# Gate and up products of two feed-forward stages by Strassen's scheme, down products in blocks of two pairs

## The chip, the cores and the metric

The kernel runs on one core of a Trainium2 chip. The metric is the device time of one execution in microseconds; the median of several runs is compared. The engines of the core are PE (TensorE: matmuls, with PEld for its weight loads), DVE (VectorE), ACT (ScalarE), POOL (GpSimd) and SP (SyncE, which issues most DMAs). Each engine executes its own instructions in a fixed order and waits on semaphores for the others.

## The reference, cut to what matters

The reference runs a two-layer block (convolutions, attentions, a mixture of 16 experts) and then a second block on 512 tokens of width 1024. The second block begins and ends with a feed-forward stage, and these two stages are what the change touches:

```python
D_MODEL = 1024; SEQ = 512; D_FF = 2816

def swiglu(x, w_gate, w_up, w_down):
    return (jax.nn.silu(x @ w_gate) * (x @ w_up)) @ w_down

def hybrid_layer(x, positions, layer_idx, ...):
    x = x + 0.5 * swiglu(rms_norm_2(x, ffn1_norm), ffn1_w_gate, ffn1_w_up, ffn1_w_down)
    ...                      # mixers
    x = x + 0.5 * swiglu(rms_norm_2(x, ffn2_norm), ffn2_w_gate, ffn2_w_up, ffn2_w_down)
    return x
```

All data are fp32. `x @ w_gate` and `x @ w_up` are each 512 x 1024 times 1024 x 2816; the product with `w_down` is 512 x 2816 times 2816 x 1024.

## The kernel before

**Precision.** A product of two fp32 matrices is made of three matmuls of a shorter type, fp32r. An operand is split into a part `hi`, which ACT makes by a copy that rounds to fp32r, and a rest `lo = x - hi`, by a subtraction on DVE or POOL (`split`, L307 to L311; `take_hl`, L253 to L265, for weights that come by DMA). `mm3` (L321 to L325) then issues hi times hi, hi times lo and lo times hi into one PSUM accumulator; its three matmuls are lines L323, L324 and L325.

**A stage** (`ffn`, L1610). The activations lie transposed in `hT`: eight blocks k of 128 channels by 512 tokens, hi and lo. `D_FF` = 2816 is 11 "pairs" p of two blocks q of 128 columns. Per pair the gate weights and the up weights come as one DMA each, 128 x 8 x 256 fp32, 1 MB. `take_hl` splits each into hi and lo, in two halves of 128 x 1024. Per block q, PE makes the gate product in a PSUM tile of pool `pd` and the up product in one of pool `pa`, each by 8 x 3 matmuls with the weights stationary (128 x 128) and 512 tokens moving. DVE scales the gate product by the row `rb` (1 / rms of each token), ACT takes the silu, DVE scales the up product and multiplies the two, and `split` leaves hi and lo in `fh` and `fl`. After 6 pairs, and again after the other 5, the down product follows: per half h of the output columns, 12 (then 10) blocks f of 128 rows of `w_down` arrive in three DMAs, and for each of 4 token tiles t, PE accumulates over all f in a PSUM tile of pool `pb`; DVE adds half of the sum to x (L1652). `along` makes `rb` on the way, in the first pair; `first_scale` also rescales x in the first stage. `rope_angles`, which the mixers need later, is issued beside the first down product of the first stage. `after(0)` and `after(1)` begin the next step (squares, transposes) when a half of x is ready.

**Which engine subtracts.** In the first stage `self.dve` is False, and the second half of each weight's `lo` is subtracted on POOL; before the second stage it is set True (`FDVE`), and DVE subtracts both halves.

**Buffers.** Weights and their hi and lo parts share the pool `wp` of 6 buffers of 8 KB per partition. `pump` (L235) lets at most `cap` = 2 weights be issued that are not yet released; `rel` releases.

**Order.** Instructions are written in program order, and a planner of the framework lays down a fixed order for each engine: it plays the program through with its own costs, and an engine that is free takes the ready instruction that stands first in the program. On the chip that order is kept, whatever the real durations.

The functions of the diff and what calls them, with the lines of the profile:

Of the kernel before, what the change touches and what calls it, by code (L numbers as in the profile page):

```python
# [6 lines left out]
F32 = mybir.dt.float32  # L7
# [62 lines left out]
YHB = 2  # L70
NEG = -1.0e30
# [46 lines left out]
class Kern:  # L118
# [327 lines left out]
    def block2_entries(self):  # L446
        def ffn(i):
            for f0, nf in ((0, 6), (6, 5)):
# [3 lines left out]
                for h in range(2):  # L452
                    r = 2 * f0 * 128
                    for n in (2 * nf - 8, 4, 4):
                        self.entries.append(([n, 512], self.a[f"f{i}d"][r:r + n * 128, h * 512:(h + 1) * 512]
                                             .rearrange("(k p) f -> p k f", p=128), "d"))
                        r += n * 128
# [1151 lines left out]

    def ffn(self, N, scale, after, beside=None):  # L1610
# [3 lines left out]
        es = self.phase(t2p=8)  # L1614
        hT = N["hT"]
        ef = self.phase(hf=1)
        fh = self.one(self.hf, (12, 512), F32R, "fh")
        fl = self.one(self.hf, (12, 512), F32R, "fl")
        rb = None
        for nf in (12, 10):  # L1620
            for p in range(nf // 2):
                Wg = self.take_hl()
                Wu = self.take_hl()
                for q in range(2):
# [4 lines left out]
                    if rb is None:  # L1629
                        rb = self.along(self.hf, scale())  # L1630
# [5 lines left out]
                    self.split(s, fh[:, 2 * p + q], fl[:, 2 * p + q], nc.vector)  # L1636
            for h in range(2):
                acc = [self.pb((2, 512)) for _ in range(2)]
                f0 = 0
                for q, n in enumerate((nf - 8, 4, 4)):  # L1640
                    W = self.take_hl()
                    if beside and (q, h) == (0, 1):
                        beside()
                        beside = None
                    for t in range(NX):
                        for f in range(n):
                            ff = f0 + f
                            self.mm3(acc[t // 2][:, t % 2], [z[:, ff, t * 128:(t + 1) * 128] for z in (fh, fl)],
                                     [w[:, f] for w in W], ff == 0, ff == nf - 1)
                        if q == 2:  # L1650
                            xs = self.xt(t)[:, h * 512:(h + 1) * 512]
                            nc.vector.scalar_tensor_tensor(xs, acc[t // 2][:, t % 2], 0.5, xs, op0=ALU.mult, op1=ALU.add)  # L1652
                    f0 += n
                    if nf == 10 and h == 1 and q == 0:
                        after(0)
# [443 lines left out]
```

## Time and profile before

| | before |
|---|---|
| median of 3 runs | 3044.39 us (3040.3, 3044.39, 3051.68) |
| profiled execution, its own time | 3035.68 us |
| its span | 3033.9 us |
| PE busy | 2839.7 us (94%) |
| DVE busy | 1276.4 us (42%) |
| ACT busy | 825.6 us (27%) |
| POOL busy | 467.5 us (15%) |
| mean granted TensorE clock | 0.97 of 2.4 GHz |

The span runs from the first to the last instruction. Busy is the time in which an engine has an instruction in work; the matmuls of PE overlap, so the distance from one matmul's start to the next, not its own duration, says how fast PE goes. The first feed-forward stage lies at about 1876 to 2220 us of the span, the second at about 2649 to 3024 us.

### The profile page before, as it was taken

How to read it: one execution, taken by the hardware profiler on the slowest of the kernel's cores; microseconds unless marked ns; L12 is line 12 of the kernel's file. 1: busy time of each engine (PE TensorE's matmuls, PEld its weight loads, DVE VectorE, ACT ScalarE, POOL GpSimd, SP SyncE). 2: the span in 40 equal slices, each digit the busy share in tenths (PEclk: the TensorE clock that was granted, in tenths of full speed). 3: DMA queues.
4: the chain of work that ended last, by engine and by line, in shares of the span. 5: the costliest groups of instructions: out<-in, count | busy, mean ns of one | idle time of the engine just before them, and what ended most of it. 6: DMA issues, size and time to landing. Idle time of an engine off the chain costs nothing.

```text
span 3033.9 us, 38589 instructions
## 1 busy us (share of the span) xinstructions
PE 2839.7 (94%) x15736; PEld 1800.9 (59%) x15736; DVE 1276.4 (42%) x2623; ACT 825.6 (27%) x1531; POOL 467.5 (15%) x380
## 2 busy tenths in 40 slices
PE   6989899999999898997999888999999999999998
PEld 3666675444444365574433224787886777788786
DVE  4387744111111157743222225532447483444344
ACT  4266432000000135631000003322236442322222
POOL 2233332111110132331000000221210001100000
PEclk9999899999999899898999999999999999999999
DMA  7710137999999842057999996222231122222222
GB/s 269 271 69 15 42 111 277 405 403 404 400 403 388 315 152 98 29 194 289 419 420 419 420 420 281 83 101 94 88 105 56 65 85 87 93 95 98 84 90 77
DMA packets 103842, 623.13 MB, mean 205 GB/s; under 512 B 11056, under 2 KB 13232, under 8 KB 36592
## 3 DMA queue, kind: packets, MB, share of 16 engines
q1 hardware_dynamic: 89120, 580.82, 48.6%
q0 software_dynamic: 8352, 18.10, 2.3%
q10 hardware_dynamic: 6192, 21.75, 1.9%
q8 instruction: 124, 2.03, 0.3%
q14 instruction: 54, 0.44, 0.0%
HBM read 601.74 MB, written 18.87 MB: 205 GB/s over the span
## 4 chain that ended last, share of the span: by engine, by line
PE 40%; DMA 11%; DVE 2%; ACT 1%; issue 0%; SPq 0%; DVEq 0%; ACTq 0%; POOLq 0%
PE pd L323 6%; PE pd L324 5%; PE pd L325 5%; DMA w<-w_up 4%; DMA w<-w_down 3%; DMA w<-w_gate 3%; PE pb L323 3%; PE pb L325 3%; PE pb L324 3%; PE pa L323 3%; PE pa L324 3%; PE pa L325 3%; PE pb L1223 2%; PE pd L1260 1%; PE pb L1791 1%; DVE wl L263 1%
## 5 line engine op out<-in xcount | busy, mean ns | idle before, releaser
L1223 PE MATMUL pb<-w,X 128*64 128x512 f32 x2048 | 463.2, 597 | 19.8 <-DMA w<-w_up 10.5
L1223 PEld LDWEIGHTS pb<-w,X 128*64 128x64 f32 x2048 | 149.5, 137 | 316.0 <-issue 265.5
L262 ACT CAST wh<-w 128x1024 fp32r<-128x1024 f32 (+3 forms) x239 | 235.8, 1028 | 367.9 <-issue 126.7
L1260 PE MATMUL pd<-w,hT 128*64 128x512 f32 (+1 forms) x2048 | 301.1, 490 | 5.2 <-DVE hT L319 2.6
L323 PE MATMUL pd<-hh,wh 128*128 128x512 f32 (+1 forms) x720 | 285.7, 397 | 10.6 <-ACT wh L262 6.4
L263 DVE TENSOR_TENSOR wl<-w,wh 128x1024 fp32r<-128x1024 f32 (+2 forms) x187 | 229.9, 1248 | 147.5 <-ACT wh L262 142.9
L324 PE MATMUL pd<-hl,wh 128*128 128x512 f32 (+1 forms) x720 | 285.1, 396 | 0.0
L325 PE MATMUL pd<-hh,wl 128*128 128x512 f32 (+1 forms) x720 | 284.2, 395 | 0.3 <-DVE wl L263 0.3
L1233 ACT ACTIVATE s<-pb 128x512 f32<-128x512 f32 x32 | 19.1, 597 | 695.8 <-PE pb L1223 695.8
L263 POOL TENSOR_TENSOR wl<-w,wh 128x1024 fp32r<-128x1024 f32 (+1 forms) x52 | 137.4, 2642 | 423.8 <-ACT wh L262 418.4
L1260 PEld LDWEIGHTS pd<-w,hT 128*64 128x64 f32 (+1 forms) x2048 | 101.9, 123 | 163.8 <-issue 129.7
L1234 DVE TENSOR_TENSOR s<-s,pb 128x512 f32<-128x512 f32 x32 | 22.0, 686 | 390.6 <-ACT s L1233 390.6
L323 PEld LDWEIGHTS pd<-hh,wh 128*128 128x128 f32 x720 | 138.7, 193 | 40.7 <-ACT wh L262 9.8
L325 PEld LDWEIGHTS pd<-hh,wl 128*128 128x128 f32 x720 | 138.9, 193 | 29.3 <-DVE wl L263 1.0
L324 PEld LDWEIGHTS pd<-hl,wh 128*128 128x128 f32 x720 | 139.3, 193 | 28.2 <-issue 1.4
L323 PE MATMUL pb<-wh,fh 128*128 128x512 f32 x352 | 139.2, 400 | 0.8 <-DVE x L1652 0.8
L323 PE MATMUL pa<-hh,wh 128*128 128x512 f32 x352 | 139.5, 396 | 0.0
L324 PE MATMUL pa<-hl,wh 128*128 128x512 f32 x352 | 139.5, 396 | 0.0
L325 PE MATMUL pa<-hh,wl 128*128 128x512 f32 x352 | 139.5, 396 | 0.0
L325 PE MATMUL pb<-wh,fl 128*128 128x512 f32 x352 | 139.2, 396 | 0.0
L324 PE MATMUL pb<-wl,fh 128*128 128x512 f32 x352 | 138.9, 395 | 0.0
L1191 POOL DMA_INDIRECT gat<-xd,gi x48 | 46.8, 974 | 575.5 <-PE pa L1205 326.5
(459 smaller groups left out, 4713.0 us busy)
## 6 DMA issues: line engine op xcount, KB each, us to landing
w<-w_up SPq DMA_DIRECT2D x128, 1024.0 KB, 17.2
w<-w_gate SPq DMA_DIRECT2D x128, 1024.0 KB, 16.8
w<-w_down SPq DMA_DIRECT2D x128, 1024.0 KB, 19.2
w<-ada_w SPq DMA_DIRECT2D x48, 1024.0 KB, 5.3
w<-w_in SPq DMA_DIRECT2D x18, 1024.0 KB, 7.0
w<-f1g SPq DMA_DIRECT2D x11, 1024.0 KB, 5.0
w<-f1u SPq DMA_DIRECT2D x11, 1024.0 KB, 4.9
w<-f2g SPq DMA_DIRECT2D x11, 1024.0 KB, 4.9
```

The source lines that it names most:

```text
L262: nc.scalar.copy(hi[:, s], w[:, s])
L263: (nc.gpsimd if i and not (dve or self.dve) else nc.vector).tensor_tensor(lo[:, s], w[:, s], hi[:, s].bitcast(F32), op=ALU.subtract)
L323: nc.tensor.matmul(ps, lhsT=l[0], rhs=r[0], start=first, stop=False)
L324: nc.tensor.matmul(ps, lhsT=l[0], rhs=r[1], start=False, stop=False)
L325: nc.tensor.matmul(ps, lhsT=l[1], rhs=r[0], start=False, stop=last)
L1191: self.nc.gpsimd.indirect_dma_start(out=g, out_offset=None, in_=R["xd"].rearrange("t (h w) -> (t h) w", h=dup), in_offset=bass.IndirectOff ...
L1223: nc.tensor.matmul(pp[h * cap:(h + 1) * cap, 0:w], lhsT=X[:, k], rhs=Wk[:, h * w:(h + 1) * w], start=(k == 0), stop=(k == 7))
L1233: nc.scalar.activation(out=s, in_=pp[:, 0, 0:w], func=AF.Silu)
L1234: nc.vector.tensor_tensor(s, s, pp[:, 1, 0:w], op=ALU.mult)
L1260: nc.tensor.matmul(py[h * cap:(h + 1) * cap, 0:w], lhsT=hT[:, k % nj, k // nj], rhs=Wd[k // 2][:, k % 2, h * w:(h + 1) * w], start=(k == 0 ...
L1791: nc.tensor.matmul(s_[:, g, :nk], lhsT=qT[0:96, h, n * 128:nk], rhs=kT[0:96, h, 0:nk], start=True, stop=False)
```

## The change

Both operands of the gate and up products are cut into quarters: the weights of a pair by k (blocks 0 to 3 and 4 to 7) and by q, the activations by k and by tokens (0 to 255 and 256 to 511). Strassen's scheme (in Winograd's form) makes the four quarters of the result of 7 products of quarters, where the direct way takes 8. Every product is 4 blocks k times 3 matmuls, 256 tokens wide.

- Pair 0 of each stage stays as it was. Beside it, `crossed` adds hi and lo of the activations to fp32 again and forms three combined quarters on POOL, which are split into hi and lo; `cross` then replaces one quarter of `hT` in place, on DVE and ACT.
- Pairs 1 to 10 go through `ffn_pair`. `seven` makes the 7 weight quarters of a matrix one after the other: four sums on POOL (128 x 512 each), and a split of each quarter, hi on ACT and lo on DVE, into a pool `pr` of 5 buffers; `sq` has 4 buffers for the sums. Gate and up products alternate. Each product goes to one half (256 columns) of a PSUM bank: four halves in two tiles per matrix, used in turn. The results are added up by ACT (the first) and DVE into four SBUF tiles of the pool `t2p`, which shrinks from 8 to 6 buffers. The two scalings by `rb` are both on the gate side, one on DVE and one, after the silu, on POOL.
- The down product follows after every second pair (and after the last alone), over 4 (the last: 2) blocks f, with one DMA of weights per half h. Its result is added to x six times in a stage instead of twice.
- `rope_angles` is issued after pair 0, `after(0)` after the first half of the last down product.

```diff
@@ -68,6 +68,9 @@
 ORATE = 1
 OCAP = 1
 YHB = 2
+SQ = 4
+PR = 5
+FT2 = 6
 NEG = -1.0e30
 TWO_PI = 6.283185307179586
 LAM_INIT = 0.8 - 0.6
@@ -445,16 +448,14 @@
 
     def block2_entries(self):
         def ffn(i):
-            for f0, nf in ((0, 6), (6, 5)):
+            for f0 in range(0, 11, 2):
+                nf = min(2, 11 - f0)
                 for p in range(f0, f0 + nf):
                     self.dense_entries(f"f{i}g", None, p, p + 1, (8, 256))
                     self.dense_entries(f"f{i}u", None, p, p + 1, (8, 256))
                 for h in range(2):
-                    r = 2 * f0 * 128
-                    for n in (2 * nf - 8, 4, 4):
-                        self.entries.append(([n, 512], self.a[f"f{i}d"][r:r + n * 128, h * 512:(h + 1) * 512]
-                                             .rearrange("(k p) f -> p k f", p=128), "d"))
-                        r += n * 128
+                    self.entries.append(([2 * nf, 512], self.a[f"f{i}d"][2 * f0 * 128:2 * (f0 + nf) * 128, h * 512:(h + 1) * 512]
+                                         .rearrange("(k p) f -> p k f", p=128), "d"))
         ffn(1)
         self.dense_entries("z0", None, 0, 2, (4, 416))
         self.dense_entries("wuq", None, 0, 1, (2, 768))
@@ -1607,18 +1608,123 @@
             nc.vector.scalar_tensor_tensor(self.xt(t), self.xt(t), r[:, t:t + 1], self.row, op0=ALU.mult, op1=ALU.mult)
         return r2
 
+    def crossed(self, N):
+        nc = self.nc
+        hi, lo = N["hi"], N["lo"]
+        T4 = self.xy.tile([128, 2, 4, 256], F32R, name=self.nm("T4"), tag="xyc", bufs=1)
+        T23 = [self.one(self.hf, (2, 4, 256), F32R, f"T{i}") for i in (2, 3)]
+        a, b = slice(0, 256), slice(256, 512)
+        for k in range(4):
+            f1, f2, c, d = (self.t2() for _ in range(4))
+            for f, kk in ((f1, k), (f2, k + 4)):
+                nc.gpsimd.tensor_tensor(f, hi[:, kk].bitcast(F32), lo[:, kk].bitcast(F32), op=ALU.add)
+            nc.gpsimd.tensor_tensor(c[:, a], f2[:, b], f1[:, b], op=ALU.subtract)
+            nc.gpsimd.tensor_tensor(f1[:, b], f1[:, b], f1[:, a], op=ALU.subtract)
+            nc.gpsimd.tensor_tensor(c[:, b], f2[:, b], f1[:, b], op=ALU.subtract)
+            nc.gpsimd.tensor_tensor(d[:, a], f2[:, a], c[:, b], op=ALU.subtract)
+            for T, z in ((T23[0], c[:, b]), (T23[1], c[:, a]), (T4, d[:, a])):
+                self.split(z, T[:, 0, k], T[:, 1, k], nc.vector)
+        return T23[0], T23[1], T4
+    def cross(self, N):
+        nc = self.nc
+        hi, lo = N["hi"], N["lo"]
+        for k in range(4):
+            f = self.t2()
+            nc.vector.tensor_tensor(f, hi[:, k].bitcast(F32), lo[:, k].bitcast(F32), op=ALU.add)
+            nc.vector.tensor_tensor(f[:, 0:256], f[:, 256:512], f[:, 0:256], op=ALU.subtract)
+            self.split(f[:, 0:256], hi[:, k, 256:512], lo[:, k, 256:512], nc.vector)
+    def seven(self, w):
+        nc = self.nc
+        A = lambda f, K: w[:, 4 * K:4 * K + 4, 128 * f:128 * f + 128]
+        s = self.one(self.sq, (4, 128), s="sq")
+        def pair(z):
+            t = self.one(self.pr, (2, 4, 128), F32R, "pr")
+            self.split(z, t[:, 0], t[:, 1], nc.vector)
+            return t
+        yield pair(A(0, 0))
+        nc.gpsimd.tensor_tensor(s, A(1, 0), A(1, 1), op=ALU.add)
+        s2 = self.one(self.sq, (4, 128), s="sq")
+        nc.gpsimd.tensor_tensor(s2, s, A(0, 0), op=ALU.subtract)
+        yield pair(s2)
+        yield pair(s)
+        yield pair(A(0, 1))
+        nc.gpsimd.tensor_tensor(A(1, 0), A(0, 0), A(1, 0), op=ALU.subtract)
+        yield pair(A(1, 0))
+        nc.gpsimd.tensor_tensor(s2, A(0, 1), s2, op=ALU.subtract)
+        yield pair(s2)
+        yield pair(A(1, 1))
+    def ffn_pair(self, N, T, rb, out):
+        nc = self.nc
+        hi, lo = N["hi"], N["lo"]
+        q = lambda K, t: [z[:, 4 * K:4 * K + 4, 256 * t:256 * t + 256] for z in (hi, lo)]
+        c = lambda z: [z[:, i] for i in range(2)]
+        rhs = [q(0, 0), c(T[0]), q(0, 1), q(1, 0), c(T[1]), q(1, 1), c(T[2])]
+        M = []
+        for pool in (self.pd, self.pa):
+            w = self.take()
+            M.append(dict(F=self.seven(w), ps=[z[:, h * 256:h * 256 + 256] for z in (pool(), pool()) for h in range(2)],
+                          r=[self.t2() for _ in range(2)]))
+        a, b = slice(0, 256), slice(256, 512)
+        add = lambda o, x, y: nc.vector.tensor_tensor(o, x, y, op=ALU.add)
+        mul = lambda o, x, y, e=nc.vector: e.tensor_tensor(o, x, y, op=ALU.mult)
+        for i in range(7):
+            for up, m in enumerate(M):
+                l = next(m["F"])
+                ps = m["ps"][i % 4]
+                for k in range(4):
+                    self.mm3(ps, [l[:, j, k] for j in range(2)], [r[:, k] for r in rhs[i]], k == 0, k == 3)
+                r0, r1 = m["r"]
+                if i == 0:
+                    nc.scalar.copy(r0[:, a], ps)
+                elif i == 1:
+                    add(r1[:, b], ps, r0[:, a])
+                elif i == 2:
+                    add(r0[:, b], ps, r1[:, b])
+                elif i == 3:
+                    add(r0[:, a], ps, r0[:, a])
+                elif i == 4:
+                    add(r1[:, a], ps, r1[:, b])
+                    add(r1[:, b], ps, r0[:, b])
+                else:
+                    h = i - 5
+                    r, c = (r0, b) if h == 0 else (r1, a)
+                    add(r[:, c], ps, r[:, c])
+                    if not up:
+                        mul(r, r, rb)
+                        nc.scalar.activation(out=r, in_=r, func=AF.Silu)
+                        mul(r, r, rb, nc.gpsimd)
+                    else:
+                        mul(r, r, M[0]["r"][h])
+                        out(h, r)
+        for m in M:
+            next(m["F"], None)
+        self.rel(2)
     def ffn(self, N, scale, after, beside=None):
 
         MARK("ffn")
         nc = self.nc
-        es = self.phase(t2p=8)
+        es = self.phase(t2p=FT2)
         hT = N["hT"]
         ef = self.phase(hf=1)
-        fh = self.one(self.hf, (12, 512), F32R, "fh")
-        fl = self.one(self.hf, (12, 512), F32R, "fl")
-        rb = None
-        for nf in (12, 10):
-            for p in range(nf // 2):
+        eo = None
+        for p in range(11):
+            if p % 2 == 0:
+                F = []
+            z = self.one(self.hf, (2, 2, 512), F32R, "fh", bufs=3)
+            F.append(z)
+            out = lambda q, s, z=z: self.split(s, z[:, 0, q], z[:, 1, q], nc.vector)
+            if p == 0:
                 Wg = self.take_hl()
                 Wu = self.take_hl()
                 for q in range(2):
@@ -1626,33 +1732,37 @@
                     for W, pp in ((Wg, pg), (Wu, pu)):
                         for k in range(8):
                             self.mm3(pp, [w[:, k, q * 128:(q + 1) * 128] for w in W], [h[:, k] for h in hT], k == 0, k == 7)
-                    if rb is None:
+                    if q == 0:
                         rb = self.along(self.hf, scale())
                     g, s = self.t2(), self.t2()
                     nc.vector.tensor_tensor(g, pg, rb, op=ALU.mult)
                     nc.scalar.activation(out=g, in_=g, func=AF.Silu)
                     nc.vector.tensor_tensor(s, pu, rb, op=ALU.mult)
                     nc.vector.tensor_tensor(s, s, g, op=ALU.mult)
-                    self.split(s, fh[:, 2 * p + q], fl[:, 2 * p + q], nc.vector)
+                    out(q, s)
+                if beside:
+                    beside()
+                T = self.crossed(N)
+                self.cross(N)
+                eo = self.phase(sq=SQ, pr=PR)
+            else:
+                self.ffn_pair(N, T, rb, out)
+            if p % 2 == 0 and p < 10:
+                continue
+            nf = 2 * len(F)
+            if p == 10:
+                eo.close()
             for h in range(2):
                 acc = [self.pb((2, 512)) for _ in range(2)]
-                f0 = 0
-                for q, n in enumerate((nf - 8, 4, 4)):
-                    W = self.take_hl()
-                    if beside and (q, h) == (0, 1):
-                        beside()
-                        beside = None
-                    for t in range(NX):
-                        for f in range(n):
-                            ff = f0 + f
-                            self.mm3(acc[t // 2][:, t % 2], [z[:, ff, t * 128:(t + 1) * 128] for z in (fh, fl)],
-                                     [w[:, f] for w in W], ff == 0, ff == nf - 1)
-                        if q == 2:
-                            xs = self.xt(t)[:, h * 512:(h + 1) * 512]
-                            nc.vector.scalar_tensor_tensor(xs, acc[t // 2][:, t % 2], 0.5, xs, op0=ALU.mult, op1=ALU.add)
-                    f0 += n
-                    if nf == 10 and h == 1 and q == 0:
-                        after(0)
+                W = self.take_hl()
+                for t in range(NX):
+                    for f in range(nf):
+                        self.mm3(acc[t // 2][:, t % 2], [F[f // 2][:, i, f % 2, t * 128:(t + 1) * 128] for i in range(2)],
+                                 [w[:, f] for w in W], f == 0, f == nf - 1)
+                    xs = self.xt(t)[:, h * 512:(h + 1) * 512]
+                    nc.vector.scalar_tensor_tensor(xs, acc[t // 2][:, t % 2], 0.5, xs, op0=ALU.mult, op1=ALU.add)
+                if p == 10 and h == 0:
+                    after(0)
         after(1)
         ef.close()
         es.close()
```

## Rows read from the trace of the kernel before

**Rows 1.** The page's busy times, and two lines of its 40 slices.

```profile
span 3033.9 us, 38589 instructions
PE 2839.7 (94%) x15736; PEld 1800.9 (59%) x15736; DVE 1276.4 (42%) x2623; ACT 825.6 (27%) x1531; POOL 467.5 (15%) x380
...
PE   6989899999999898997999888999999999999998
...
PEclk9999899999999899898999999999999999999999
```

**Rows 2.** Busy time by windows: stretch, length, busy (count), clock, DMA share, GB/s.

```profile
2672.00:2694.40 22.40, 22.40 (x97) 17.99 (x97) 9.99 (x13) 6.30 (x8) 0.00 (x0) 1.00 0.27 94
...
1876.00:2220.00 344.00, 342.15 (x1468) 274.00 (x1469) 148.28 (x192) 101.25 (x144) 77.39 (x31) 1.00 0.26 90
2649.00:3024.00 375.00, 374.22 (x1609) 299.54 (x1607) 157.84 (x207) 98.98 (x131) 0.00 (x0) 1.00 0.25 87
```

**Rows 3.** Windows, PE alone: a run of 48 matmuls 256 columns wide.

```profile
359.27:365.04 5.77, 5.77 (x50) 1.00 0.00 0
```

**Rows 4.** Groups by form, second stage (2649 to 3024): busy, mean ns, idle before.

```profile
L263 DVE TENSOR_TENSOR wl<-w,wh 128x1024 fp32r<-128x1024 f32 x63 | 75.2, 1221 | 38.9 <-ACT wh L262 38.8
...
L323 PE MATMUL pd<-hh,wh 128*128 128x512 f32 x176 | 69.8, 397 | 0.0
...
L323 PE MATMUL pb<-wh,fh 128*128 128x512 f32 x176 | 69.6, 399 | 0.8 <-DVE x L1652 0.8
...
L323 PEld LDWEIGHTS pd<-hh,wh 128*128 128x128 f32 x176 | 33.2, 188 | 7.9
...
L1635 DVE TENSOR_TENSOR t<-t,t 128x512 f32<-128x512 f32 x22 | 15.2, 692 | 2.3
...
L311 DVE TENSOR_TENSOR fl<-t,fh 128x512 fp32r<-128x512 f32 x22 | 15.1, 688 | 7.6 <-ACT fh L310 7.6
L1633 ACT ACTIVATE t<-t 128x512 f32<-128x512 f32 x22 | 13.8, 629 | 48.2 <-DVE t L1632 48.2
L310 ACT CAST fh<-t 128x512 fp32r<-128x512 f32 x22 | 13.6, 618 | 58.6 <-DVE t L1635 58.6
L1652 DVE SCALAR_TENSOR_TENSOR x<-pb,x 128x512 f32<-128x512 f32 x15 | 10.4, 691 | 34.9 <-PE pb L325 34.9
```

**Rows 5.** Groups by form, whole span, DVE: 256 columns, one source in PSUM.

```profile
L1234 DVE TENSOR_TENSOR s<-s,pd 128x256 f32<-128x256 f32 x16 | 6.7, 421 | 13.9 <-ACT s L1233 13.9
```

**Rows 6.** Line L1029: durations in ns, smallest, median and largest, on POOL.

```profile
L1029 POOL TENSOR_TENSOR xc<-xc,t x3: 1274/1276/1291, 463.0 to 479.2; 128x512 f32<-128x512 f32 x3
```

**Rows 7.** Timeline of DVE in the first stage: start, length, operation.

```profile
1929.52 0.69 DVE L1635 TENSOR_TENSOR t<-t,t 128x512 f32<-128x512 f32 x1
1930.13 1.22 DVE L263 TENSOR_TENSOR wl<-w,wh 128x1024 fp32r<-128x1024 f32 x1
1931.27 2.89 DVE L311 TENSOR_TENSOR fl<-t,fh 128x512 fp32r<-128x512 f32 x1
1934.35 0.69 DVE L1632 TENSOR_TENSOR t<-pd,along 128x512 f32<-128x512 f32 x1 [0.19 <-PE pd L325]
```

**Rows 8.** Timeline of POOL in the same stretch.

```profile
1930.67 2.94 POOL L263 TENSOR_TENSOR wl<-w,wh 128x1024 fp32r<-128x1024 f32 x1 [3.18 <-ACT wh L262]
```

**Rows 9.** Timeline of DVE beside a busy POOL, first block.

```profile
197.83 0.73 DVE L631 SCALAR_TENSOR_TENSOR y<-u,hb,y 128x499 f32<-128x499 f32 x1
198.47 0.28 DVE L319 COPY y<-pa 128x128 f32<-128x128 f32 x1
198.68 0.81 DVE L839 TENSOR_REDUCE ng<-pb 128x1 f32<-128x640 f32 x1
```

**Rows 10.** Timeline of POOL there.

```profile
197.96 1.54 POOL L627 TENSOR_TENSOR a<-a,tap 128x509 f32<-128x509 f32 x1
```

**Rows 11.** Groups by form, first stage (1876 to 2222), POOL.

```profile
L263 POOL TENSOR_TENSOR wl<-w,wh 128x1024 fp32r<-128x1024 f32 x28 | 74.4, 2657 | 243.6 <-ACT wh L262 243.6
```

**Rows 12.** The page's DMA issues: count, KB each, median us to landing.

```profile
w<-f1g SPq DMA_DIRECT2D x11, 1024.0 KB, 5.0
```

## The prediction

> **What bounds the kernel now.** I read the page first: of a span of 3033.9 us PE is busy 2839.7 [rows 1]. Then the windows of the two stages: PE is busy 342.15 of 344.00 us in the first and 374.22 of 375.00 in the second, with the clock granted in full [rows 2]. The groups name what ends PE's idle time there: 0.8 us for the x update, next to nothing else [rows 4]. So both stages are PE's own stream; time taken from it shortens the span one for one, as long as nothing else becomes late. One pair is the window of 22.40 us: 96 matmuls (the count shows one neighbour more), with DVE busy 9.99 us, ACT 6.30, POOL 0 [rows 2]. PE is the only engine without slack, and the change buys PE time with work on the other three.
>
> **PE.** A pair issues 2 x 2 x 8 x 3 = 96 matmuls of 512 columns, 22.40 / 96 = 233 ns apart. Afterwards it issues 2 x 7 x 4 x 3 = 168 of 256 columns. Their pace is in the trace: a run of 48 fills 5.77 us, 120 ns each [rows 3] (two neighbours overlap the edges of that window). 168 x 0.120 = 20.2 us, so a pair saves 2.2 us where the bare count, an eighth, gives 2.8. Ten pairs in two stages: 20 x 2.2 = 44 us. The down products keep their 528 matmuls of 512 columns a stage (176 for each line of `mm3` [rows 4]): 96 x 0.233 = 22.4 us for a block of two pairs.
>
> **What the others get, per pair.** DVE, 512 columns, both sources in SBUF: 14 `lo` parts of weight quarters, 2 scalings, 2 products of silu and up, 2 `lo` parts of the result, 20 in all. Such an instruction takes 692 or 688 ns [rows 4], and the next starts 0.61 us after it (1929.52 to 1930.13 [rows 7]): 12.2 us. DVE, 256 columns with one source in PSUM: 7 additions per matrix, 14, of 421 ns [rows 5], 0.34 with the same overlap of 0.08: 4.8 us. So 17.0 us of 20.2. ACT: 18 instructions of 512 columns at 618 to 629 ns [rows 4], about 11 us, never the bound. POOL: 8 sums and 2 scalings of 512 columns at 1276 ns [rows 6], 12.8 us; that the sums read the weights in four pieces no row shows, and I take the contiguous price. The weight quarters' hi and lo are made from five buffers, so five products can lie ready, 7.2 us of PE's work.
>
> **DVE and POOL shut each other out.** At 1930.67 POOL begins a subtraction while DVE has one in work until 1931.35; POOL's ends at 1933.61, 2.26 us after DVE's. DVE's next, `lo` of the result, begins at 1931.27 and lasts 2.89 us instead of 0.69: it ends 0.55 us after POOL's [rows 7, 8]. So two-source instructions in SBUF run one at a time. A DVE instruction that reads PSUM is not held: the copy at 198.47 and the reduction at 198.68 are done in 0.28 and 0.81 us beside a POOL addition that lasts to 199.50 [rows 9, 10]. A POOL instruction of 512 columns therefore takes about 1.13 us (half of 2.26) from DVE, unless DVE has an addition out of PSUM just then. Today this costs nothing: POOL has 28 such subtractions in the first stage [rows 11], and PE is idle there for 1.85 us in all [rows 2].
>
> **A block of two pairs and its down product**, as it repeats four times a stage. PE: 40.4 + 22.4 = 62.8 us; before, 67.2. In the down product DVE and POOL can work ahead: five quarters of the next pair (five buffers) and that pair's 8 sums on POOL (four buffers and one in place). For the 40.4 us of the pairs there remain on DVE 35 two-source instructions x 0.61 = 21.4, the first down weights' `lo` 2 x 1.14 = 2.3 (1221 ns [rows 4], 1.14 to the next [rows 7]), 28 additions x 0.34 = 9.5: 33.2 us. On POOL: the second pair's 8 sums and 4 scalings, 12 x 1.13 = 13.6. If nothing overlaps, 46.8; if all additions fall beside POOL, 37.3, less than PE's 40.4. These are the two ends, 40.4 and 46.8. I take the middle, 42.0, and for PE's wait at the end of each pair for one turn of POOL and DVE, 1.13 + 0.61 = 1.7, so 43.7: 3.3 more than PE alone. 8 blocks: +26 us. In the first stage one of the two `lo` halves of the first down weights is POOL's (2.26 instead of 1.14): 4 x 1.1, +4.
>
> **Pair 0 and `crossed`.** On POOL: 4 blocks k of 2 additions of 512 columns and 4 of 256: 4 x (2 x 1.28 + 4 x 0.7) = 21.4 us, the 0.7 being half of rows 6 and a little. It starts when the activations are complete, in the second stage about when pair 0 starts, and then come the 4 sums that pair 1's second products need, 4 x 1.28 = 5.1; with 4 us for DVE's own turns, 30.5 us. PE comes there after pair 0 and three products, 22.4 + 3 x 1.44 = 26.7, and the split of the sum takes 0.62 + 0.69 [rows 4]: 5 to 7 us late. I take 7 in the second stage and 4 in the first, where pair 0 is drawn out by the transposes: +11. If POOL gets ahead, 0. `cross` (DVE, ACT) and `rope_angles` lie within that wait.
>
> **The rest.** Down products start with three blocks f that are ready and have 4 tiles t to choose from, so the last block's chain (addition 0.42, product 0.69, hi 0.62, lo 0.69, 2.4 us) has cover from 9 to 36 matmuls (2.1 to 8.4 us): 0. The last pair of a stage has only its own two blocks, and `after(0)` has 5.6 us instead of 11: +2 per stage, +4. The x update rises from 16 to 48 instructions of 691 ns [rows 4], 32 x 0.61 = 20 us more DVE time, within the down products, which hold DVE for little else. DMA: the same bytes; a load lands in 5.0 us [rows 12] and each has over 10 us between the release of a buffer and its use: 0, and 5 us for each load that lost this cover.
>
> **Sum.** -44 + 26 + 4 + 11 + 4 = +1 us on the profiled execution's 3035.7. That one lies 8.7 us below the median of the three runs, 3044.4; on the median's scale, 3046 us. So I forecast no change that can be told from none: POOL and DVE, taking turns, give back what PE saves. What can be told is about 0.5%, 15 us.
>
> **Rivals.**
>
> A, the work ahead covers it. The blocks run at PE's 40.4 us, `crossed` costs half: -44 + 5.5 + 4 = -34 us, 3010. For it: DVE has idle time today even in the pair's window (9.99 of 22.40), and additions out of PSUM run beside POOL [rows 9, 10]. Against: 33.2 + 13.6 us of turns for 40.4.
>
> B, slower, by the halves of a bank. Products 3 and 4 of a matrix (and 5 and 6) write the two halves of one bank. If PE may not write one half while DVE still reads the other, product 4 waits for the addition of product 3, and between them lies only the other matrix's product, 1.44 us. The addition takes 0.42, but on DVE it stands behind a two-source instruction that waits for POOL, 0.61 + 1.13 = 1.74: 0.7 us late. At products 5 and 6 two additions stand in the way, 0.76: 1.06 late. Two matrices: 3.5 us a pair, and it decides from 2.2 a pair on, where the saving is gone. A block's pairs then take 2 x 23.7 = 47.4, 7.0 over PE: 8 x 7.0 = 56 in place of 26, and 4 x 3.5 for the pairs that stand alone: +1 + 30 + 14 = +45 us, 3089. No row shows a bank read in one half and written in the other, so nothing here excludes it. The Trainium skill ("PSUM — Partial Sum Buffer", section "PSUM bank collisions raise a hardware error") says that a matmul's write and another engine's read of one bank collide even at different columns, and that software must guard by bank; by that rule the wait of B exists, and only its length is open. No run so far shows it.
>
> C, the change does not do what it says, as 256 columns would be bound by the load of the weights. A load shows 188 ns [rows 4]; were that the pace, a pair would take 31.6 us. The 120 ns of rows 3 exclude it, with the same 128 x 128 weights.
>
> **How the numbers follow.** Forecast 0.36, with 3030 to 3062 as its own range; A 0.33; B 0.31; C none. The forecast's spread gives 0.05 to each side. Faster by over 0.5%: 0.38; within: 0.26; slower: 0.36. The range of 3002 to 3095 leaves out a tenth at each end: below, A with `crossed` free; above, B with both ends of the blocks bad.
>
> **What would show it.** Right: matmuls of 256 columns 120 ns apart within a product; DVE two-source instructions of 512 columns at 1.5 to 1.9 us in the pairs' windows, each ending half a microsecond after POOL's; PE idle 1 to 2 us a pair, ended by `lo` parts on DVE. Wrong: PE at 100% in the pairs (A); idle time ended by additions out of PSUM, before products 4 and 6 (B); a long wait at pair 1 of over 10 us, or waits for DMA.

## The result, and the profile after

The changed kernel takes 3199.4 us (median of four runs, 3194.3 to 3201.5) against 3043.9: ratio 1.0505, 95% interval 1.0481 to 1.0529. It is 5% slower, 155 us where +1 was forecast, and outside the range of 3002 to 3095. The page of the changed kernel, beside [rows 1]:

```profile
span 3192.4 us, 42851 instructions
PE 2854.2 (89%) x17176; PEld 1874.2 (59%) x17176; DVE 1636.4 (51%) x3195; ACT 934.4 (29%) x1803; POOL 770.0 (24%) x608
...
PEclk9998999999999898989999997999999999899999
```

PE is busy 14 us longer although its work became less, and the span grew by 158 us: PE waits, and its clock is granted in full less often. Where: the two stages by windows, from pair 0's run of matmuls to the last down product. (In the kernel before, these are 1876 to 2258 and 2654.5 to 3024; the 2220 given ahead as the end of the first is too early.) The columns are those of [rows 2] (stretch, length, then busy time of PE, PEld, DVE, ACT, POOL, granted clock, DMA share, GB/s). First the kernel before, then the changed one:

```profile
1876.00:2258.00 382.00, 380.15 (x1641) 304.29 (x1642) 159.58 (x206) 113.79 (x167) 82.36 (x35) 1.00 0.27 94
2654.50:3024.10 369.60, 368.82 (x1578) 295.08 (x1576) 152.57 (x199) 94.79 (x125) 0.00 (x0) 1.00 0.24 85
```

```profile
1876.00:2342.00 466.00, 388.77 (x2345) 342.45 (x2346) 344.77 (x474) 160.44 (x289) 206.88 (x139) 0.91 0.20 71
2745.40:3180.10 434.70, 370.65 (x2298) 327.04 (x2296) 320.82 (x465) 148.54 (x257) 174.80 (x124) 0.94 0.20 73
```

The stages took 84 and 65 us more, 149 of the 158. PE's waits name two places (the second stage; what waited for what, total, times, longest):

```profile
PE pb L326 <- ACT fh L313: 22.0, 9, 4.4
PE pd L326 <- ACT hh L313: 20.3, 1, 20.3
PE pb L328 <- DVE fh L314: 5.8, 6, 1.5
PE pd L328 <- DVE pr L314: 4.8, 4, 1.2
PE pd L326 <- DVE t L1677: 3.0, 8, 0.5
```

`pb <- fh` is the start of a down product: it waits for the result of the pair just done. `pd <- hh`, once a stage, is pair 1, waiting for what `cross` writes into `hT`. Neither group waited in the kernel before [rows 4].

One block of two pairs with its down product, in the second stage. The windows: the pairs' products; the down product until the first wait ends; the stretch behind it; the rest.

```profile
2921.40:2964.60 43.20, 40.33 (x323) 38.95 (x322) 38.48 (x59) 20.84 (x34) 14.43 (x10) 1.00 0.21 75
2964.60:2969.40 4.80, 1.56 (x8) 0.94 (x6) 3.64 (x7) 1.27 (x3) 3.41 (x3) 0.91 0.53 208
2969.40:2976.60 7.20, 6.79 (x17) 5.10 (x17) 6.03 (x6) 3.38 (x6) 5.86 (x4) 0.59 0.00 0
2976.60:2996.00 19.40, 19.38 (x89) 15.74 (x90) 7.24 (x11) 0.89 (x2) 6.86 (x5) 1.00 0.29 109
sum 74.60, PE 68.06 PEld 60.73 DVE 55.41 ACT 26.38 POOL 30.55; mean PE 17.01 PEld 15.18 DVE 13.85 ACT 6.59 POOL 7.64
```

The block takes 74.6 us; PE alone needs 62.8. Of the 11.8 us between them some 5 are lost in the pairs, and some 7 at the change from pairs to down product: PE runs six matmuls, waits 3.28 us, and then 7.2 us go by at a mean granted clock of 0.59. Why `fh` is late, from the timelines of DVE, then of POOL, then of ACT (start, length, operation, idle before):

```profile
2963.41 1.78 DVE L1678 TENSOR_TENSOR t<-t,along 128x512 f32<-128x512 f32 x1
2965.11 0.41 DVE L1677 TENSOR_TENSOR t<-pa,t 128x256 f32<-128x256 f32 x1
...
2965.78 1.11 DVE L314 TENSOR_TENSOR pr<-w,pr 128x512 fp32r<-128x512 f32 x1
2968.04 0.69 DVE L1678 TENSOR_TENSOR t<-t,t 128x512 f32<-128x512 f32 x1 [1.16 <-POOL t L1678]
...
2969.59 0.68 DVE L314 TENSOR_TENSOR fh<-t,fh 128x512 fp32r<-128x512 f32 x1
2971.43 1.75 DVE L1678 TENSOR_TENSOR t<-t,t 128x512 f32<-128x512 f32 x1 [1.17 <-POOL t L1678]
2973.10 1.76 DVE L314 TENSOR_TENSOR pr<-w,pr 128x512 fp32r<-128x512 f32 x1
2974.79 1.78 DVE L314 TENSOR_TENSOR fh<-t,fh 128x512 fp32r<-128x512 f32 x1
```

```profile
2962.47 2.16 POOL L1654 TENSOR_TENSOR sq<-sq,w 128x512 f32<-128x512 f32 x1
2964.59 1.75 POOL L1658 TENSOR_TENSOR w<-w 128x512 f32<-128x512 f32 x1
2966.30 1.71 POOL L1678 TENSOR_TENSOR t<-t,along 128x512 f32<-128x512 f32 x1
2970.07 1.33 POOL L1678 TENSOR_TENSOR t<-t,along 128x512 f32<-128x512 f32 x1 [2.07 <-ACT t L1703]
2971.37 1.26 POOL L1652 TENSOR_TENSOR sq<-w 128x512 f32<-128x512 f32 x1
2972.71 1.61 POOL L1654 TENSOR_TENSOR sq<-sq,w 128x512 f32<-128x512 f32 x1
2974.28 1.74 POOL L1658 TENSOR_TENSOR w<-w 128x512 f32<-128x512 f32 x1
```

```profile
2965.22 0.64 ACT L1703 ACTIVATE t<-t 128x512 f32<-128x512 f32 x1 [3.55 <-DVE t L1678]
```

The pair's last matmul is issued at 2964.5. The chain from there (scaling on DVE, silu, scaling on POOL L1678, product, hi, lo, for each of two blocks q) ends its last `lo` at 2976.57, 12.1 us later. POOL's sums for the next pair (L1652 to L1658) run between its links. They hardly delay POOL's own link: the silu ends at 2965.86, and the scaling starts at 2966.30, after the sum L1658. They delay DVE: two-source instructions that start beside them take up to 1.78 us, most of them 1.75, instead of 0.69. Two of these (1.11 and 1.76 us) are `lo` parts of the next pair's weights (`pr`), which the fixed order puts between the links. An addition out of PSUM beside the sum of 2964.59 takes 0.41 us, as the prediction said. The Trainium skill ("SBUF — State Buffer", section "SBUF: two separate sides") has this as an exclusive lock: of a GpSimd instruction that reads SBUF and a DVE instruction with two SBUF inputs, the one that starts first has it for its whole length, and the other is fully blocked. The trace agrees: the product of 2971.43 starts 0.06 us after the sum of 2971.37 to 2972.63, and ends 0.55 us after it, at 2973.18.

### The profile page after: what moved, and what is told of

The parts are those of the page before. It is cut to its first block, busy times and chain, and to the rows that moved or that the text cites. A ratio compares the mean times of both kernels' runs of the same rounds, so it can differ in the third digit from the quotient of the medians.

```text
span 3192.4 us, 42851 instructions
## 1 busy us (share of the span) xinstructions
PE 2854.2 (89%) x17176; PEld 1874.2 (59%) x17176; DVE 1636.4 (51%) x3195; ACT 934.4 (29%) x1803; POOL 770.0 (24%) x608
## 5 line engine op out<-in xcount | busy, mean ns | idle before, releaser
L326 PE MATMUL pb<-wh,fh 128*128 128x512 f32 x352 | 151.9, 436 | 46.5 <-ACT fh L313 45.5
L266 DVE TENSOR_TENSOR wl<-w,wh 128x1024 fp32r<-128x1024 f32 (+3 forms) x127 | 168.7, 1342 | 40.5 <-ACT wh L265 35.8
L326 PE MATMUL pd<-hh,wh 128*128 128x512 f32 (+1 forms) x400 | 159.1, 399 | 9.2 <-ACT wh L265 6.4
L327 PE MATMUL pd<-hl,wh 128*128 128x512 f32 (+1 forms) x400 | 158.6, 396 | 1.8 <-DVE hl L1561 1.8
L328 PE MATMUL pd<-hh,wl 128*128 128x512 f32 (+1 forms) x400 | 157.4, 394 | 0.3 <-DVE wl L266 0.3
L314 DVE TENSOR_TENSOR pr<-w,pr 128x512 fp32r<-128x512 f32 x160 | 144.6, 912 | 24.4 <-ACT pr L313 23.1
L328 PE MATMUL pb<-wh,fh 128*128 128x512 f32 x352 | 145.5, 424 | 8.9 <-DVE fh L314 8.8
L628 POOL TENSOR_TENSOR a<-a,tap 128x505 f32<-128x505 f32 (+13 forms) x86 | 104.5, 1216 | 165.0 <-ACT tap L626 159.7
L326 PE MATMUL pd<-hh,pr 128*128 128x256 f32 x320 | 94.2, 294 | 53.3 <-ACT hh L313 40.3
L326 PE MATMUL pd<-wh,hh 128*128 128x512 f32 (+2 forms) x320 | 127.5, 402 | 6.2 <-ACT wh L265 5.8
L327 PE MATMUL pd<-wl,hh 128*128 128x512 f32 (+2 forms) x320 | 127.0, 398 | 3.5 <-DVE wl L266 2.4
```

The lines of the kernel that those rows point to most:

```text
L266: (nc.gpsimd if i and not (dve or self.dve) else nc.vector).tensor_tensor(lo[:, s], w[:, s], hi[:, s].bitcast(F32), op=ALU.subtract)
L314: (eng or nc.gpsimd).tensor_tensor(lo, src, hi.bitcast(F32), op=ALU.subtract)
L326: nc.tensor.matmul(ps, lhsT=l[0], rhs=r[0], start=first, stop=False)
L327: nc.tensor.matmul(ps, lhsT=l[0], rhs=r[1], start=False, stop=False)
L328: nc.tensor.matmul(ps, lhsT=l[1], rhs=r[0], start=False, stop=last)
L628: nc.gpsimd.tensor_tensor(a2[:, to], a2[:, to], f, op=ALU.add)
```

## Experiments

All are edits of the changed kernel unless another is named; ratios are against the kernel before, with 95% intervals. Differences between two edits are those of their medians; by the ratios they come out up to 7 us different.

### Is it the order of the down product?

**e1: the first pair's blocks f for all tiles first.**

```
-  for t in range(NX):
-      for f in range(nf): ...
+  for p0 in range(0, nf, 2):
+      for t in range(NX):
+          for f in range(p0, p0 + 2): ...
```

> Only the order of PE's work in the down products changes: the two blocks f of the first pair for all four tiles t, and only then those of the second pair (24 matmuls, 5.6 us, ahead of the first one that needs the last pair's result, where the changed kernel has 6, 1.4 us). Theory (the start of the down product): the waits of 3.3 to 4.4 us for `fh` vanish at 10 of 12 starts, and with them the stretches at half clock behind them, together 8 to 12 us a block: 3199 - 90 = about 3110 us. Rival (DVE and POOL are full, and any cover is used up by the next wait): the time moves into the pairs, at most 20 us are won, 3180.

3216.9 us, 1.0567 (1.0550 to 1.0585): 17 us slower than the changed kernel, so both theories failed. Its down product by windows:

```profile
2909.90:2916.40 6.50, 6.50 (x29) 4.92 (x27) 4.67 (x8) 2.38 (x4) 4.43 (x4) 1.00 0.46 161
2916.40:2922.10 5.70, 1.24 (x4) 0.52 (x3) 5.16 (x4) 2.27 (x4) 5.00 (x4) 0.68 0.00 0
2922.10:2929.00 6.90, 5.90 (x14) 4.17 (x15) 3.88 (x5) 0.00 (x0) 3.35 (x2) 0.52 0.00 0
```

PE runs 24 matmuls at full clock, and then waits all the same, 5.5 us in three pieces. The chain ends 12.2 us after the pair's last matmul, as before the edit: it outlasts a cover of 5.6 us as it outlasts 1.4. In the changed kernel PE works through part of the chain, at half clock; here it idles until the chain ends and has the half-clock stretch (0.52) after it. The three windows and the rest of the down product, 14.4 us, make 33.5 us where the changed kernel takes 31.4: 2.1 more here, 14 in the eight blocks that repeat, most of the 17.

**e7: 16 matmuls that nobody reads, ahead of the first late one** (`nc.tensor.matmul(acc[1][:, 1], lhsT=F[0]..., rhs=W[0]...)`, in the first half of each down product).

> In each down product's first half, behind the six matmuls that need no late result, 16 matmuls of 512 columns are added whose result nobody reads (3.7 us, weights and activations that are ready): PE works through the wait. Theory (the wait costs twice: 3.3 us, and then the clock falls to its lower level for some 6 us): the clock stays up behind the wait, 10 starts x 4 to 5 us: 3199 - 45 = about 3155 us. Rival (the half clock has another cause, or only idle time counts): 3195 to 3210.

3253.3 us, 1.0692 (1.0674 to 1.0710), 54 us slower: a miss. The fill lasts 3.7 us, the chain 12: PE still waits 5.7 us behind it in each block of the second stage, and the clock still falls. The 16 take the place of useful work: by the chain's end the changed kernel has issued 22 of the down product's 96 matmuls, e7 only 11, and the others come after it, in part at half clock. The down product takes 38.0 us. The fill was sized by the wait, not by the chain, so this run doesn't tell what the half clock costs.

**e3: all pairs direct, in the new blocks.** (`if p == 0:` becomes `if True:`; no `crossed`, `cross` or `ffn_pair`.)

> All pairs computed directly as before the change, in the new blocks of two pairs with the changed kernel's down products: the change of blocks alone. Theory (the start of the down product is late by itself, as only 6 matmuls stand ahead of the last pair's result): 1 to 2 us and some half clock at each of 12 starts, 20 to 50 us slower than before: 3064 to 3094. Rival (the start is late only because POOL and DVE are held by the sums and splits): 3044 to 3054.

3073.9 us, 1.0101 (1.0084 to 1.0118): the blocks alone cost 30 us. In the second stage, where POOL does nothing, a block takes 68.4 us against 67.2 of PE's work; in the first, where POOL subtracts half of each `lo`, 71.4, with 1.9 us of waiting for `fh` each time. So the theory's 20 to 50 us are right, but that is a fifth of the loss, and most of it lies in the stage in which POOL works.

### Is it POOL?

**e5: the gate's second scaling by `rb` on DVE. e15: the 8 sums of a pair on DVE. e6: both.**

```
-  mul(r, r, rb, nc.gpsimd)                      # e5, e6
+  mul(r, r, rb)
-  nc.gpsimd.tensor_tensor(s, A(1, 0), ...)      # all four lines of seven(): e15, e6
+  nc.vector.tensor_tensor(s, A(1, 0), ...)
```

> The gate's second multiplication by `rb`, two POOL instructions a pair, goes to DVE; POOL keeps the 8 sums. Theory (the chain at the end of a pair is long because it takes turns with POOL in its middle): the wait of 3.3 us before the down product shrinks by 1 to 2 us, and the half clock behind it by 1 to 2 us, at 10 starts: 3199 - 30 = about 3170 us. Rival (DVE is simply full, every instruction more counts): 20 x 2 x 0.61 = 24 us more, of which the part in the pairs is seen: 3200 to 3215.

> The changed kernel with the 8 sums of a pair on DVE; POOL keeps the two scalings by `rb`. Theory (the next pair's sums stand in front of the scaling on POOL and hold DVE in turns while the chain wants both): most of the 119 us that both moves gave, 3095 to 3115. Rival (the scaling on POOL, in the middle of the chain, is what costs): no more than 40 to 60 us, 3140 to 3160.

> Sums and scalings all on DVE: POOL has nothing to do in the pairs (it keeps `crossed`). Theory (DVE and POOL shut each other out, so POOL's help is worth nothing): DVE's instructions come down from a mean of 0.91 to 0.69 us, the chain before the down product gets shorter, pairs stay at 43 to 45 us a block: 3140 to 3190 us. Rival (POOL's share is real relief): DVE has 23.1 us of work a pair against PE's 20.2, a block's pairs take 46 to 48 us instead of 43.1: +30 to 50, 3230 to 3250.

e5: 3171.7 us, 1.0437 (1.0413 to 1.0460), as its theory in time. e15: 3112.0, 1.0232 (1.0212 to 1.0253), as its theory. e6: 3080.6, 1.0137 (1.0114 to 1.0160), 119 us less, twice what its theory allowed. Of the 119 the sums alone give 87 and the scalings alone 28; the two nearly add up. The chain from a pair's last matmul to the last `lo`, in a block of the second stage, goes the same way: 12.1 us in the changed kernel, 10.2 in e5, 8.3 in e15, 5.4 in e6. A block of e6 in the second stage takes 64.2 us:

```profile
2839.10:2903.30 64.20, 63.20 (x434) 58.30 (x434) 57.12 (x100) 26.26 (x44) 0.00 (x0) 1.00 0.27 99
```

DVE does 100 instructions where it did 80, and is busy 57.1 us where it was 55.4 and POOL 30.5. The 20 that came over cost DVE 1.7 us: it had been spending the rest of their time in turns with POOL. The rival, that POOL relieved DVE, counted 23.1 us of DVE a pair against PE's 20.2; over a block with its down product that fits.

**e12 and e8: e6 with pair 1 direct, and that with e1's order.**

> All on DVE and pair 1 direct, but the down products in the changed kernel's order: the order's own worth once POOL is out. Theory (chain of 4 to 6 us after the pair's last matmul, cover 1.4 us against 5.6): 1 to 2 us of waiting at 10 starts more than with the order, 3060 to 3070 us. Rival (the order is worth nothing): 3045 to 3052.

> Three edits together: sums and scalings on DVE, the down products' order with 24 matmuls ahead of the last pair's result, pair 1 direct. Theory (the order alone won nothing because the chain, stretched by POOL's turns, takes 12 us after the pair's last matmul, more than the cover of 5.6): without POOL the chain is 4 to 6 us and fits: the starts cost nothing, blocks take 46 + 22.4 us or less: about 3080 to 3110 us. Rival (the order itself is worse): the kernel with all on DVE minus the 36 us of pair 1, plus 17.

e12: 3053.4, 1.0045 (1.0029 to 1.0061), nearer its rival than its theory. e8: 3049.6, 1.0020 (1.0008 to 1.0033), better than its theory's 3080. The order that cost 17 us with POOL in the chain now gives 4 to 8 (the intervals touch, so its sign is barely told), less than the 10 or more expected: e6's chain of 5.4 us is nearly short enough for the old order too.

### Pair 1

**e2: pair 1 direct** (`if p < 2:`, `cross` after it). **e4: the same with e1's order.**

> Pair 1 of each stage is computed directly like pair 0, so that the seven products start with pair 2 and `crossed` has a pair and a down product more of PE's work beside it. Theory (`crossed` is late): the two waits of 20 us at pair 1 vanish with some 2 to 4 us of half clock behind each; the pair gives back 2.2 us a stage: 3199 - 40 = about 3158 us. Rival (POOL's 18 us are only moved, and lock DVE during pair 1's own chain and the first down product): half of it, 3180.

> Both edits: the down products' order of the first kernel, pair 1 direct as in the second. Theory: the two losses are separate and add: about 3110 - 40 = 3070 us or less; what is left over the sum of PE's own work (3044 - 40) is DVE and POOL within the pairs. Rival: no more than the better of the two alone, 3110 or above.

e2: 3163.1, 1.0393 (1.0375 to 1.0410), 36 us less, as its theory in time. But its first down products wait 15.0 and 7.8 us (the longest, 9.1, for hi of the down weights), so part of the wait was only moved, as the rival said. e4: 3186.2, 1.0466 (1.0449 to 1.0483): each edit adds roughly its own effect, and e1's is a loss, so the theory's 3070 was not reached.

**e13: `crossed` on DVE. e16: `crossed` on POOL with temporaries of its own.**

```
-  f1, f2, c, d = (self.t2() for _ in range(4))
+  f1, f2, c, d = (self.one(self.xp, (512,), s="xt") for _ in range(4))   # a pool of 12
```

> The changed kernel with one edit: `crossed` on DVE instead of POOL. Theory (POOL's turns with DVE make it late): 16 us of DVE in a row, the wait of 20 us at pair 1 falls under 8 us in both stages, and the half clock behind it goes: 3199 - 30 = about 3170 us. Rival (it is the order: buffers held until splits that stand behind pair 0's work, and `cross` last): the wait stays at 15 to 20 us, 3190 to 3200.

> The changed kernel with one edit: `crossed` takes its four temporaries a block from a pool of 12 of its own and not from the 6 that it shares with pair 0's chain. Theory (it starts late because it waits for buffers): it begins when the activations are complete, about 10 us earlier, and the wait at pair 1 falls from 20 to 8 to 12 us in both stages: 3199 - 20 = about 3178 us. Rival (POOL's pace, its turns with DVE and the place of `cross` behind it set the end): 3190 to 3200.

e13: 3188.2, 1.0486 (1.0464 to 1.0508): the longest wait is still 13.9 us, so its rival, the order, is nearer. e16: 3191.4, 1.0479 (1.0441 to 1.0517), the rival's time, but not for the rival's reason: here the wait itself is gone, and the time hardly moved. Waits around pairs 0 and 1 of the second stage in e16:

```profile
PE pb L326 <- ACT wh L265: 6.5, 1, 6.5
PE pb L1573 <- DVE rsy L282: 4.0, 1, 4.0
PE pb L326 <- ACT fh L313: 3.9, 2, 3.5
...
PE pd L326 <- ACT hh L313: 1.1, 1, 1.1
```

20.3 us became 1.1, so buffers made `crossed` late. But begun at once it runs beside pair 0 (POOL 2757.5 to 2780.7, the splits on DVE), and pair 0's row `rb` is copied (L1576) 21.8 us after the activations are complete where it was 8.9: PE waits for `rb` and the down weights instead. POOL in the changed kernel shows the buffers:

```profile
2757.38 1.73 POOL L1660 TENSOR_TENSOR sq<-w,sq 128x512 f32<-128x512 f32 x1
2759.07 2.54 POOL L1622 TENSOR_TENSOR t<-hh,hl 128x512 f32<-128x512 f32 x2
...
2770.43 3.91 POOL L1622 TENSOR_TENSOR t<-hh,hl 128x512 f32<-128x512 f32 x2 [4.47 <-DVE t L1741]
```

The activations were complete at 2749.4. `crossed` starts (L1622) at 2759.1, behind all 8 sums of pair 1, and its second block k at 2770.4, after a product of pair 0 (L1741) let a buffer go.

### A faster kernel

**e9: e8 with both `lo` halves on DVE in the first stage too** (`take_hl(dve=True)` in `ffn`). **e10: e9 with `crossed` on DVE. e11: e10 with one block f at a time through the tiles.**

> The kernel with three edits (all on DVE, order of the down products, pair 1 direct), and in the first stage DVE also subtracts the second half of each weight's `lo`, which POOL did there. Theory (what makes a block of the first stage 65.5 us long and one of the second 62.9 is POOL's turns): 4 x 2.6 = 10 us less, 3040 us. Rival (DVE has no room for four more subtractions a block beside its 46 us): no gain, 3050.

> As the one above, and `crossed` on DVE instead of POOL: no two-source work on POOL is left in the stages. Theory (`crossed` on POOL locks DVE during pair 1's chain, hence the wait of 9.1 us before the first down product of stage 1 and of 3.2 us in stage 2, with half clock behind it): 10 to 15 us less than the one above, about 3027 us. Rival (16 us more on DVE beside pair 1 make pair 1's own chain as late as POOL did): no change.

> As the one above, and the down products run one block f at a time through the four tiles (36 matmuls ahead of the last block's result in a block of two pairs, 12 in the last pair, where there were 24 and 6). Theory: only the single pair at the end of each stage still waits, 2.4 to 3.3 us; half of that and of the half clock behind it goes: 4 to 8 us less, about 3020 us, clearly faster than before the change. Rival: the x updates of the four tiles come at once at the end and delay the next half: no change or +5.

e9: 3032.6, 0.9966 (0.9952 to 0.9980). e10: 3013.1, 0.9917 (0.9899 to 0.9934), 0.8% faster than the kernel before (25 us by the ratio, 30 by the medians) and 186 us faster than the changed one. e11: 3016.4, 0.9912 (0.9897 to 0.9927), the same as e10. A block of e10, whole and cut at the end of the pairs:

```profile
2774.60:2837.40 62.80, 62.80 (x434) 58.38 (x433) 57.18 (x101) 26.26 (x44) 0.00 (x0) 1.00 0.27 101
2774.60:2812.70 38.10, 38.10 (x319) 38.10 (x318) 35.68 (x69) 21.23 (x35) 0.00 (x0) 1.00 0.23 83
2812.70:2837.40 24.70, 24.70 (x117) 20.29 (x116) 21.49 (x34) 5.03 (x9) 0.00 (x0) 1.00 0.33 128
```

PE never idles: 62.8 us, the number that the prediction gave PE alone.

**e14: e10 with pair 1 by seven products again. e17: that with e16's pool.**

> The best kernel so far (3013 us: all two-source work on DVE, new order of the down products, pair 1 direct) with pair 1 by seven products again. Theory (with `crossed` on DVE only 22 us of DVE stand between pair 0 and pair 1, PE comes after 26.7): the two pairs' 2.2 us come in, 3009 us. Rival (late by the order, as above): two waits of 10 to 20 us and half clock behind them, 3035 to 3060.

> The same pool in the kernel with pair 1 by seven products and all two-source work on DVE (3052 us). Theory (buffers): `crossed` is done beside pair 0, and only `cross` is left, which may overwrite the quarters only after pair 0's last matmul, 4 x 1.5 = 6 us against 2.9 us of products: the waits of 9 and 15 us fall to 3 to 6, 3052 - 18 = about 3034 us, still behind pair 1 direct (3013). Rival (DVE's own amount of work beside pair 0): 3045 to 3055.

e14: 3052.3, 1.0039 (1.0025 to 1.0053), 39 us slower than e10, as its rival. e17: 3034.1, 0.9968 (0.9951 to 0.9986), as its theory in time, but the waits left are not those that it named: with its own buffers and no POOL none for what `cross` writes is in the trace; waits for `fh` (10.2 us in all, the longest 6.9) and for `pr` (14.4) stand in its place. It is 21 us behind e10, where pair 1 by seven products could save 4.4.

## Why the prediction was wrong, point by point

- **PE: right.** Matmuls of 256 columns are 119 to 120 ns apart, and e10's block takes the 62.8 us of the working. Of the 18 pairs x 2.2 = 40 us that e10 could save it keeps 25 to 30.
- **DVE and POOL shut each other out: right in kind, and read from the right rows.** 0.69 us became 1.75 beside POOL's sums, each ending 0.55 us after POOL's, as forecast. But the prediction used it only for the throughput of a block's pairs, and there it was near in the second stage: 43.2 us against 38.1 in e10 with four matmuls fewer, 4.6 lost where 3.3 were forecast. (The forecast's 42.0 is the middle of 37.3 and 46.8, not of the two ends that it names, 40.4 and 46.8; that would be 43.6, and 13 us more over 8 blocks.) In the first stage a block's pairs took 45.6 to 49.1 us: 7 to 10.5 lost, where 4.4 were forecast. Some 4 of these a block are the waits of rival B, below.
- **"Down products start with three blocks f that are ready ...: 0": the step that failed.** It priced the last block's chain at 2.4 us, as unlocked instructions with nothing between them. It left out that the gate's chain comes first (scaling, silu, a scaling on POOL), for two blocks q, and that POOL's next sums, allowed to work ahead, take turns with all of it. Measured: 12.1 us (10.6 in the first stage). Without POOL it is 5.4 (e6), so of the 9.7 that were missing 3.0 are the links left out and 6.7 come with POOL's work. A down product took 31.4 us against 24.7 in e10: 54 us in the eight blocks that repeat. With POOL out, the 0 is nearly right: e6 has a cover of 1.4 us, and its second stage waits 1.00 a block. The cover was also two blocks f and not three, but e1 shows that more does not help against 12 us.
- **`crossed`, +11: failed in its start.** The forecast let it begin when the activations are complete. It began 9.6 us later, its second block 21 us later (buffers shared with pair 0, sums of pair 1 first), and `cross` came last. Two waits of 20 us with half clock behind them: e2 puts the net at 36 + 4.4 = about 41 us, part of the wait being only moved there.
- **Rivals.** A was excluded by the lock for the changed kernel, but it is nearly what e10 does: work ahead covers all once POOL is out. B's wait exists, with the mechanism of the prediction. In the first stage the gate's product 4 waits for the addition of product 3 in the other half of the bank:

```profile
2102.65 0.41 DVE L1677 TENSOR_TENSOR t<-pd,t 128x256 f32<-128x256 f32 x1
2103.21 0.36 PE L326 MATMUL pd<-hh,pr 128*128 128x256 f32 x1 [2.34 <-DVE t L1677]
```

  The waits for L1677 are 12.9 us over both stages. Another 8.6 are of the same kind, one that B did not name: product 2 waits until ACT has copied product 1 out of the other half (L1687). That makes 21.5 where B has 3.5 for each of 20 pairs, 70; the long ones, of about 2 us, come once each in a block of the first stage, and e10 has neither: DVE or ACT must be late first. The Trainium skill's rule (guard PSUM by bank, "PSUM — Partial Sum Buffer", section "PSUM bank collisions raise a hardware error") agrees with this wait. C was rightly excluded. DMA cost nothing, as forecast: no wait of PE in the stages ends at one.
- **The clock: not in the sum at all.** No step asked how PE runs after a wait. At the starts of the changed kernel's down products a fall of the clock cost nothing on top (last section); in e1 it does.
- **Where the 155 us are.** Stretch by stretch against e10: the eight blocks that repeat take 73.0 to 80.2 us instead of 62.8, 110 us in all where the forecast has 30. The two first blocks (pairs 0 and 1 with their down product) take 69 us more, 73 with the 4.4 that pair 1 by seven products saves, where the forecast has 11. The last pairs take 4 more, beside the 2 us of waiting at the end of each stage that e10 has too. Over the forecast that is 80, 62 and some 4; another 9 lie outside the two stages and stay unexplained.

Of the signs that the prediction named, those for it are there in the second stage: DVE's instructions of 1.75 us, and waits of PE in the pairs that end with `lo` parts. So are two that it listed as proof against it: the wait of over 10 us at pair 1, and, in the first stage, those before product 4.

## What to carry to other kernels

Work given to POOL is not free when DVE has two-source work in SBUF at the same time: count it as DVE time first (here the 20 POOL instructions of a block, 30.5 us, cost DVE 1.7 us of busy time once it did them), and don't let it work ahead beside a chain that PE waits for. Before calling a chain covered, walk it link by link with everything that its engines may put between, in the durations under contention, and compare that with the cover. Temporaries of a new step that come from a pool in use decide when the step starts.

## What the runs showed of the hardware that had not been expected

What a wait of PE does to the clock, and what that costs, can't be told from the wait's length. Behind the wait of 3.28 us the matmuls of 512 columns stood some 430 ns apart instead of 233, at a granted clock of 0.50, the 1.2 GHz level (PE's timeline):

```profile
2972.16 0.63 PE L326 MATMUL pb<-wh,fh 128*128 128x512 f32 x1
2972.59 0.63 PE L327 MATMUL pb<-wl,fh 128*128 128x512 f32 x1
```

One block earlier PE waits 3.34 us at the same place, and the clock stays in full. The same down product, until the chain ends and from there on:

```profile
2890.00:2902.00 12.00, 5.93 (x25) 3.95 (x23) 9.67 (x12) 4.64 (x8) 9.30 (x7) 1.00 0.22 84
2902.00:2921.40 19.40, 19.35 (x88) 15.72 (x89) 7.28 (x11) 0.89 (x2) 6.84 (x5) 1.00 0.29 109
```

It too takes 31.4 us. At full clock PE is through with what is ready sooner, and waits again until the chain ends; so the half clock costs nothing there on top of the chain. It costs where it comes after the chain, as in e1 (0.52 for 6.9 us). Behind a wait of 1.87 us in e3's first stage the granted clock was 0.50 from 2075 to 2077 us; behind one of 1.00 us in e6 (PE's timeline, then the windows) it stayed in full:

```profile
2885.29 0.50 PE L326 MATMUL pb<-wh,fh 128*128 128x512 f32 x1 [1.00 <-DVE x L1763]
```

```profile
2882.60:2899.60 17.00, 16.00 (x71) 12.54 (x70) 15.29 (x24) 2.28 (x4) 0.00 (x0) 1.00 0.51 186
```

And DVE can be filled far: 57.2 us of 62.8 in e10's block without one wait of PE, with POOL silent.
